# Pairs of feature tiles of the up projection by seven half-width block products, and sums of weights by adding DMAs

## The chip, the cores and the metric

The kernel runs on one core of one Trainium2 chip. The metric is the device time of one execution in microseconds (us). Five engines take part: TensorE (PE) multiplies matrices and loads its weights, VectorE (DVE) and ScalarE (ACT) work on elements, GpSimd (POOL) works on elements and can issue DMAs, SyncE (SP) issues most DMAs. Data lies in DRAM, in the on-chip memory SBUF, and in PSUM, to whose eight banks matmuls write.

## The reference

One post-norm layer of an encoder over 512 tokens of width 1024, in fp32. A combined projection of x feeds a bidirectional state-space branch and a dilated attention branch; both are projected back, gated and mixed, and the sum goes through a layer norm. The result, h1 here, enters the channel sublayer, which alone the change touches:

```python
h = layer_norm(alpha * h + mix, ln1_g, ln1_b)
f = jnp.square(jax.nn.relu(h @ w_up)) @ w_down
h = layer_norm(alpha * h + f, ln2_g, ln2_b)
```

w_up is 1024 × 4096, w_down is 4096 × 1024.

## The kernel before

fp32 products are made from three matmuls on split operands: each operand is a high part (a cast to the type fp32r, done by ACT) and a low part (the difference, done by DVE), and high × high, high × low and low × high are summed in PSUM.

**Up projection.** h1 is transposed (`h1_transpose`, L941 on) into `hth` and `htl`, high and low part, as eight K tiles of 128 features by 512 tokens. The 4096 features of the layer are 32 tiles of 128, in four chunks `ch` of eight tiles `b`. `up_block(ch, b)` makes one tile: `up_mm` issues 24 matmuls (eight K tiles, three products each) of 512 columns into one bank, through `quarters` (L141), with the weights stationary; then ACT takes relu (L993) and the square (L994) into r. The first half of tiles 0 to 3 of chunk 0 is made earlier, between the transposes, with 256 columns. The weights come from `Stream`: SP loads 512 KB per tile (`wraw`, three buffers, L89), ACT casts `wh` (L110), DVE subtracts `wl` (L111); wh and wl have two buffers each.

**Down projection.** For chunks 0 to 2 each chunk's part is a product of 2 × 2 blocks made by the seven products of Winograd's form of Strassen's method. `SEQ` gives their order, 1, 5, 6, 7, 3, 2, 4; `product` (L151 to L153) issues 24 matmuls of 512 columns for each. Some operands are sums of blocks: `sums` makes those of the activations (L1027) and those of the weights (L1030), both on DVE and in place in a block whose own use is over; `split` then makes high and low parts of activations (`ah`, `al`, L1036, L1037) and of weights (`ch`, `cl`, L1042, L1043), two buffers each. The weight blocks are four quarters of 1 MB (`wq`), loaded by `load_quarters` on SP. Chunk 3 is multiplied plainly at the end.

**Order.** In the loop one tile of chunk ch + 1 alternates with one product of chunk ch. All engines run their own queue in order; the program's text and a scheduler with priorities set those orders, and semaphores tie the queues together. A `tile_pool` with n buffers under one tag makes the writer of buffer n + 1 wait for the readers of the first.

The loop of before, in which the change lies:

```python
    for ch in range(3):
        for n, p in enumerate(SEQ):
            up_block(ch + 1, UP_ORDER[1][n])
            product(ch, p, ops)
            if n < 6:
                ops = prepare(ch, n + 1)
```

Of the kernel before, what the change touches and what calls it, by code (L numbers as in the profile page):

```python
# [45 lines left out]
def hybrid_layer_kernel(ctx: ExitStack, tc: tile.TileContext, t: dict, out: bass.AP):  # L46
# [29 lines left out]

    class Stream:
        def __init__(self):
            self.srcs, self.raw, self.hl, self.n = [], {}, {}, 0

        def add(self, ap, width=1024, hold=None):
            self.srcs.append((ap, width, hold))

        def load(self, i):
            if i < len(self.srcs) and i not in self.raw:
                ap, width, hold = self.srcs[i]
                r = wp.tile([P, 1024], F32, name=f"wraw{i}", tag="wraw", bufs=3)
                if i:
                    dma.dma_start(r[:, :width], ap)  # L89
                else:  # L90
                    act.dma_start(r[:, :512], ap[:, :512])
                    dma.dma_start(r[:, 512:width], ap[:, 512:])
                self.raw[i] = r

        def prep(self, i):
            if i < len(self.srcs) and i not in self.hl:
                self.load(i)
                ap, width, hold = self.srcs[i]
                if hold and hold[0] not in held:
                    return  # L100
                r = self.raw[i]
                if hold:
                    h = held[hold[0]].tile([P, 1024], F32R, name=f"wh{i}", tag=f"h{hold[1]}", bufs=1)
                    l = held[hold[0]].tile([P, 1024], F32R, name=f"wl{i}", tag=f"l{hold[1]}", bufs=1)
                else:
                    h = wp.tile([P, 1024], F32R, name=f"wh{i}", tag="wh", bufs=2)
                    l = wp.tile([P, 1024], F32R, name=f"wl{i}", tag="wl", bufs=2)
                with tc.high_priority(PRIO):
                    if i:
                        act.copy(h[:, :width], r[:, :width])  # L110
                        dve.tensor_sub(l[:, :width], r[:, :width], f32(h[:, :width]))  # L111
# [787 lines left out]
    for ch in range(4):  # L899
        for b in UP_ORDER[ch > 0]:  # L900
            if ch or b >= NU:
                ws.add(t["w_up"][ch * 8 + b])
# [52 lines left out]
    pre = []
# [44 lines left out]
    qp = wq_ctx.enter_context(tc.tile_pool(name="qp", bufs=1, side="right", reuse_waits="tile"))  # L1000
    quarter = {}

    def load_quarters(ch):
        for half, c in ((0, 0), (0, 1), (1, 1), (1, 0)):
            q = qp.tile([P, 2, 1024], F32, name=f"wq{ch}_{half}{c}", tag="wq", bufs=4)
            for j in range(2):
                dma.dma_start(q[:, j, :], t["w_dn"][ch // 2, c, (ch % 2) * 4 + half * 2 + j])
            quarter[ch, half, c] = q

    SEQ = [1, 5, 6, 7, 3, 2, 4]  # L1010

    def operands(ch, p):

        b11, b12, b22, b21 = [quarter[ch, *x] for x in ((0, 0), (0, 1), (1, 1), (1, 0))]
        lo, hi = slice(0, 256), slice(256, 512)
# [4 lines left out]
        w = {1: (b11, None), 5: (b11, (b12, b11)), 6: (b11, (b22, b11)), 7: (b12, (b22, b12)),  # L1020
             3: (b22, None), 2: (b21, None), 4: (b11, (b21, b11))}[p]
        return a, w

    def sums(ch, p):
        (a, asum), (w, wsum) = operands(ch, p)
        if asum:
            dve.tensor_tensor(a, asum[0], asum[1], op=asum[2])  # L1027
        if wsum:
            for j in range(2):
                dve.tensor_sub(w[:, j, :], wsum[0][:, j, :], wsum[1][:, j, :])  # L1030
# [206 lines left out]
```

## Time and profile before

| | |
|---|---|
| median of three runs | 1001.0 us (1000.8 to 1001.79) |
| profiled execution, span from first to last instruction | 999.2 us |
| the median lies above that span by | 1.8 us |
| PE busy | 988.5 us, 99 % |
| DVE busy | 742.2 us, 74 % |
| ACT busy | 553.6 us, 55 % |
| POOL busy | 51.3 us, 5 % |
| moved by DMA | 140.43 MB |
| granted TensorE clock | 0.998 |

The profile is one execution. The page gives busy times of the engines, the chain of waits that ended last, and groups of instructions by line; windows give the same for a stretch of time, and the timeline single instructions. A group's row reads: line, engine, operation, output <- inputs, shapes, count | busy us, mean ns of one | idle time of the engine just before them, and what ended it. A row of waits reads: who waited <- for whom: us in total, times, the longest. A row of the chain reads: start in us, length in us, engine, tile, line, count. A row of DMAs reads: destination <- source, the queue, count, size, median us from issue to landing.

The stage that the change touches lies, in that execution, between about 650 us (transposes of h1) and 948 us. The loop's three chunks begin at 708.8, 790.6 and 872.2.

### The profile page before, as it was taken

To read this page: it belongs to the slowest core of one execution; us is meant where nothing else is said; L and a number is where in the kernel's file an instruction comes from. 1 tells how busy PE (TensorE), PEld (TensorE's weight loads), DVE (VectorE), ACT (ScalarE), POOL (GpSimd) and SP (SyncE) were. 2 spreads that over 40 slices of the span, in tenths; PEclk is the share of its full clock that TensorE was granted. 3 is DMA by queue.
4 is the path that set the end of the run, shared out by engine and by line. 5 is a ranking of instruction groups with operands and counts; after the bars stand their busy time and mean duration, and the time that the engine had idled before them with its cause. 6 is when DMAs were issued, how large, how long until landed. Compare 5 with 4: busy or idle time off the path is not lost.

```text
span 999.2 us, 13445 instructions
## 1 busy us (share of the span) xinstructions
PE 988.5 (99%) x4967; PEld 820.6 (82%) x4967; DVE 742.2 (74%) x1120; ACT 553.6 (55%) x1031; POOL 51.3 (5%) x50
## 2 busy tenths in 40 slices
PE   9999999999999999999999999999999999999997
PEld 7888888888887888788778888898888888888886
DVE  4296997789998998895787267564775876787457
ACT  4454796469766984884774343134543545455330
POOL 0000100120012002102000000000000000000000
PEclk9999999999999999999999999999999999999999
DMA  7445376335653574484764258234224224321222
GB/s 243 153 134 167 105 216 196 96 118 153 204 148 113 165 221 123 119 256 142 250 204 117 75 189 312 68 101 153 73 96 153 80 72 145 100 61 45 85 85 85
DMA packets 53202, 140.43 MB, mean 141 GB/s; under 512 B 7056, under 2 KB 8208, under 8 KB 52880
## 3 DMA queue, kind: packets, MB, share of 16 engines
q1 hardware_dynamic: 52992, 139.30, 44.6%
q8 instruction: 39, 0.64, 0.3%
q10 hardware_dynamic: 144, 0.26, 0.1%
q14 instruction: 27, 0.22, 0.1%
HBM read 128.25 MB, written 11.30 MB: 140 GB/s over the span
## 4 chain that ended last, share of the span: by engine, by line
PE 96%; DVE 3%; ACT 0%; issue 0%; DVEq 0%; ACTq 0%
PE ps_u L141 18%; PE ps_pa L141 9%; PE ps_z L141 9%; PE ps_x L141 9%; PE ps_g L141 7%; PE ps_p L153 4%; PE ps_p L152 4%; PE ps_p L151 4%; PE ps_q L141 3%; PE ps_k L141 3%; PE ps_B L141 2%; PE ps_yo L526 2%; PE ps_C L141 2%; PE ps_d L152 1%; PE ps_d L151 1%; PE ps_d L153 1%
## 5 line engine op out<-in xcount | busy, mean ns | idle before, releaser
L111 DVE TENSOR_TENSOR wl<-wraw,wh 128x1024 fp32r<-128x1024 f32 (+1 forms) x141 | 173.6, 1235 | 140.7 <-ACT wh L110 114.8
L110 ACT CAST wh<-wraw 128x1024 fp32r<-128x1024 f32 (+1 forms) x141 | 146.1, 1040 | 195.1 <-PE ps_u L141 100.6
L141 PE MATMUL ps_u<-hth,wh 128*128 128x512 f32 (+1 forms) x272 | 101.4, 377 | 0.2 <-ACT hth L951 0.2
L141 PE MATMUL ps_u<-hth,wl 128*128 128x512 f32 (+1 forms) x272 | 101.2, 377 | 0.0
L1043 DVE TENSOR_TENSOR cl<-wq,ch 128x1024 fp32r<-128x1024 f32 x42 | 51.2, 1222 | 33.0 <-ACT ch L1042 33.0
L151 PE MATMUL ps_p<-ch,ah 128*128 128x512 f32 x168 | 65.4, 389 | 0.0
L152 PE MATMUL ps_p<-cl,ah 128*128 128x512 f32 x168 | 65.4, 389 | 0.0
L153 PE MATMUL ps_p<-ch,al 128*128 128x512 f32 x168 | 65.4, 389 | 0.0
L141 PE MATMUL ps_u<-htl,wh 128*128 128x512 f32 (+1 forms) x272 | 63.8, 377 | 0.0
L141 PEld LDWEIGHTS ps_u<-hth,wh 128*128 128x128 f32 x272 | 51.2, 188 | 9.8 <-ACT hth L951 0.5
L141 PEld LDWEIGHTS ps_u<-hth,wl 128*128 128x128 f32 x272 | 51.2, 188 | 9.4
L141 PEld LDWEIGHTS ps_u<-htl,wh 128*128 128x128 f32 x272 | 49.2, 188 | 9.4
L1042 ACT CAST ch<-wq 128x1024 fp32r<-128x1024 f32 x42 | 44.1, 1051 | 16.9 <-PE ps_p L153 16.9
L141 PE MATMUL ps_pa<-yh,wh 128*128 128x512 f32 x128 | 51.7, 404 | 0.0
L141 PE MATMUL ps_g<-xh,wh 128*128 128x512 f32 x128 | 51.5, 402 | 0.0
L141 PE MATMUL ps_z<-xh,wh 128*128 128x512 f32 x128 | 50.7, 396 | 0.0
L141 PE MATMUL ps_x<-xh,wh 128*128 128x512 f32 x128 | 50.4, 394 | 0.0
L141 PE MATMUL ps_z<-xl,wh 128*128 128x512 f32 x128 | 49.9, 390 | 0.0
L141 PE MATMUL ps_g<-xl,wh 128*128 128x512 f32 x128 | 49.9, 390 | 0.0
L141 PE MATMUL ps_x<-xl,wh 128*128 128x512 f32 x128 | 49.8, 389 | 0.0
L141 PE MATMUL ps_pa<-yl,wh 128*128 128x512 f32 x128 | 48.4, 393 | 0.0
L314 DVE SCALAR_TENSOR_TENSOR acc<-ps_x,vec,acc 128x510 f32<-128x510 f32 (+1 forms) x64 | 47.6, 744 | 0.8 <-ACT acc L312 0.3
(298 smaller groups left out, 2331.8 us busy)
## 6 DMA issues: line engine op xcount, KB each, us to landing
wraw<-in_w_in_dram SPq DMA_DIRECT2D x68, 512.0 KB, 3.7
bc<-dr_acr SPq DMA_DIRECT2D x64, 256.0 KB, 4.4
wraw<-in_w_up_dram SPq DMA_DIRECT2D x32, 512.0 KB, 3.6
wq<-in_w_dn_dram SPq DMA_DIRECT2D x24, 512.0 KB, 4.4
be<-dr_ear SPq DMA_DIRECT2D x32, 256.0 KB, 5.4
wraw<-in_w_ps_dram SPq DMA_DIRECT2D x16, 512.0 KB, 3.8
dr_gate<-g SPq DMA_DIRECT2D x16, 256.0 KB, 2.1
wraw<-in_w_out_dram SPq DMA_DIRECT2D x8, 512.0 KB, 4.6
```

The costliest lines, as they stand in the source:

```text
L110: act.copy(h[:, :width], r[:, :width])
L111: dve.tensor_sub(l[:, :width], r[:, :width], f32(h[:, :width]))
L141: ins = pe.matmul(ps, l, r, start=(first and n == 0), stop=(last and n == len(seq) - 1))
L151: pe.matmul(ps, lh, rh, start=(first and i == 0), stop=False)
L152: pe.matmul(ps, lh, rl, start=False, stop=False)
L153: ins = pe.matmul(ps, ll, rh, start=False, stop=(last and i == n - 1))
L314: dve.scalar_tensor_tensor(acc[:, o0:o1], ps[:, i0:i1], w(k), acc[:, o0:o1], op0=ALU.mult, op1=ALU.add)
L526: pe.matmul(po[d][:, ch(c)], prev[d, c][:, pr * P:(pr + 1) * P], C[:, ch(c)], start=True, stop=True)
L1042: act.copy(h, w[:, j, :])
L1043: dve.tensor_sub(l, w[:, j, :], f32(h))
```

## The change

**Up projection.** Tiles 0 to 7 (chunk 0) stay. Tiles 8 to 31 become twelve pairs (`PAIRS`: chunks 1 to 3, tiles 4 and 5, 6 and 7, 0 and 1, 2 and 3). A pair's product (512 tokens × 1024 by 1024 × 256 features) is seen as 2 × 2 blocks: A11 and A12 are K tiles 0 to 3 and 4 to 7 of the first 256 tokens, A21 and A22 the same of the last 256; B11 and B21 are the K halves of the pair's first tile, B12 and B22 of its second. It is made by seven products `qmul` of 12 matmuls of 256 columns, in four segments (`up_seg`):

- seg 0: x = A11·B11, y = A12·B21; C11 = x + y
- seg 1: z = S1·T1, x += S2·T2
- seg 2: x += S3·T3, z += S4·B22; C22 and C12 come from z, x and copies taken in between
- seg 3: x += A22·T4; C21 = x

with S1 = A21 − A22, S2 = S1 − A11, S4 = A12 + S2, S3 = A11 − A21, and T1 = B11 + B12, T3 = B12 + B22, T2 = T1 + B22, T4 = B21 + T2. The S are made once, in `act_sums` on DVE and ACT during chunk 0, from `hf`, an unsplit copy of h1 transposed (eight more copies on ACT, L957); S3 overwrites A21.

**Sums by DMA.** T1, T3, T2 and T4 are made in the raw weight buffers of a pair by four adding DMAs of 256 KB on POOL's queue (L1063, L1067, L1068, L1070; called adds A, B, C, D in this order), then split by `wsplit` (L1049 casts on ACT, subtractions on DVE) into three operand buffers. The third add may only start when T1 has been read, since it overwrites it. The weight sums of the down projection's products 5, 6, 7 and 4 become adding DMAs of 1 MB on POOL's queue (L1171); the signs of the activation sums and of some additions change with it.

**Order.** The order of PE in the loop is written out by hand: for the first pair of a chunk (q = 0) seg 0, seg 1, a product, seg 2, a product; for the next two seg 3 of the pair before, seg 0, half a product, seg 1, the other half, seg 2, a product; for the last seg 3, seg 0, half a product, seg 1, the other half, seg 2, seg 3. Products use two pairs of banks instead of three. The weight quarters' pool opens later, when `hf` is closed.

```diff
+    def act_sums():
+        a11, a12, a21, a22 = hf[:, 0:4, LO], hf[:, 4:8, LO], hf[:, 0:4, HI], hf[:, 4:8, HI]
+        s3 = fp.tile([P, 4, S], F32, name="s3", tag="r1", bufs=2)[:, :, LO]
+        dve.tensor_sub(s3, a11, a21)
+        dve.tensor_sub(a22, a21, a22)
+        act_split("S1", a22)
...
+    def pair_prep(n, e):
+
+        if n >= len(PAIRS):
+            return
+        r0, r1 = raw_w[n, 0], raw_w.get((n, 1))
+        if e == 0:
+            h, l = slot(f"pa{n}")
+            wsplit(h, l, r0)
+            op_w[n, "B11"], op_w[n, "B21"] = (h, l, K0), (h, l, K1)
+            pool.dma_start(r0[:, K0], r1[:, K0], accum_op=ALU.add)
+        elif e == 1:
+            h, l = slot(f"pb{n}")
+            wsplit(h[:, K0], l[:, K0], r0[:, K0])
+            pool.dma_start(r1[:, K0], r1[:, K1], accum_op=ALU.add)
+            pool.dma_start(r0[:, K0], r1[:, K1], accum_op=ALU.add)
+            wsplit(h[:, K1], l[:, K1], r0[:, K0])
+            pool.dma_start(r0[:, K1], r0[:, K0], accum_op=ALU.add)
+            op_w[n, "T1"], op_w[n, "T2"] = (h, l, K0), (h, l, K1)
...
+    def qmul(ps, a, n, w, first):
+        src, k0, cs = mov[a]
+        h, l, ws_ = op_w.pop((n, w))
+        seq = [(h, x, k) for k in range(4) for x in range(2)] + [(l, 0, k) for k in range(4)]
+        for i, (w_, x, k) in enumerate(seq):
+            wk = slice(ws_.start + k * P, ws_.start + (k + 1) * P)
+            pe.matmul(ps[:, LO], w_[:, wk], src[:, x, k0 + k, cs], start=(first and i == 0), stop=(i == 11), skip_group_check=not first)
...
     def sums(ch, p):
-        (a, asum), (w, wsum) = operands(ch, p)
+        (a, asum), (w, wadd) = operands(ch, p)
         if asum:
             dve.tensor_tensor(a, asum[0], asum[1], op=asum[2])
-        if wsum:
-            for j in range(2):
-                dve.tensor_sub(w[:, j, :], wsum[0][:, j, :], wsum[1][:, j, :])
+        if wadd is not None:
+            pool.dma_start(w, wadd, accum_op=ALU.add)
...
-    BANKS = [(0, 1), (3, 4), (5, 2)]
+    BANKS = [(0, 1), (3, 4)]
...
+    with tc.manual_schedule(engines={mybir.EngineType.PE}):
+        for c in range(3):
+            for q in range(4):
+                n = c * 4 + q
+                if q:
+                    up_seg(n - 1, 3)
+                up_seg(n, 0)
+                pair_prep(n, 2)
+                if q == 0:
+                    up_seg(n, 1)
+                    pair_prep(n, 3)
+                pr = product(c, SEQ[2 * q], ops)
+                next(pr)
+                if q:
+                    up_seg(n, 1)
+                    pair_prep(n, 3)
+                for _ in pr:
+                    pass
+                if q < 3:
+                    ops = prepare(c, 2 * q + 1)
+                pair_prep(n + 1, 0)
+                up_seg(n, 2)
```

On PE, at the boundary from chunk 0 to chunk 1 of the loop, the order of before has whole tiles (the end of tile 3 of chunk 1 and the beginning of tile 4 of chunk 2, whose weights are wh118 and wl118; rows that only repeat are left out):

```order
L141 MATMUL ps_u1_3_7266<-htl_6044,wh117_7196 128x512 x8
L141 MATMUL ps_u2_4_7315<-hth_6043,wh118_7269 128x512 [waits Activation_49]
L141 MATMUL ps_u2_4_7315<-hth_6043,wl118_7270 128x512 [waits DVE_49]
L141 MATMUL ps_u2_4_7315<-hth_6043,wh118_7269 128x512
L141 MATMUL ps_u2_4_7315<-hth_6043,wl118_7270 128x512
```

and the order of the change, at the same place, has seg 3 of pair 3 (pd3), seg 0 of pair 4 (pa4), seg 1 of pair 4 (pb4 holds T1 and T2) and product 1 of chunk 1 (here too without the rows that repeat):

```order
L1089 MATMUL ps_x3_7418<-ht_6049,pd3h_7497 128x256 [waits DVE_49]
L1089 MATMUL ps_x3_7418<-ht_6049,pd3l_7498 128x256 x4
L1089 MATMUL ps_x4_7600<-ht_6049,pa4h_7517 128x256 x8
L1089 MATMUL ps_y4_7613<-ht_6049,pa4h_7517 128x256 x8
L1089 MATMUL ps_z4_7636<-S1_6556,pb4h_7590 128x256 [waits DVE_49,Activation_49]
L1089 MATMUL ps_z4_7636<-S1_6556,pb4l_7591 128x256 [waits DVE_49]
L1089 MATMUL ps_x4_7600<-S2_6560,pb4h_7590 128x256 [waits Activation_49]
L1089 MATMUL ps_x4_7600<-S2_6560,pb4l_7591 128x256 [waits DVE_49]
L148 MATMUL ps_p11_3_7671<-ch110_7580,ah11_7576 128x512
```

The wait of a tile for its weights became two waits a product apart, and the product of T2 follows that of T1 with nothing between.

On ACT, at the same boundary, before (ch and ah are weights and activations of products 1 and 5 of chunk 1; wh119 and wh120 are weights of later tiles):

```order
L1042 CAST ch110_7303<-wq1_00_7254 128x1024 [waits DMAHW0_49,DVE_49,PE_49]
L1042 CAST ch111_7307<-wq1_00_7254 128x1024 [waits DMAHW1_49,DVE_49,PE_49]
L110 CAST wh119_7318<-wraw119_7194 128x1024 [waits DMAHW5_49,PE_49]
L993 ACTIVATE r1_0_7044<-ps_u1_3_7266 128x512
L994 ACTIVATE r1_0_7044<-r1_0_7044 128x512 [waits Activation_49]
L1036 CAST ah11_7299<-r1_0_7044 128x1024 [waits Activation_49]
L1036 CAST ah15_7380<-r1_0_7044 128x1024 [waits DVE_49]
L110 CAST wh120_7398<-wraw120_7267 128x1024 [waits DMAHW0_49,PE_49]
```

and with the change (pb4h is cast twice: first its half T1, in the first row, and last its half T2; pc4h is T3|B22; DMASW are semaphores of POOL's DMAs):

```order
L1049 CAST pb4h_7590<-pr4_0_7293 128x512 [waits DMASW4_49,PE_49]
L1102 ACTIVATE r1_0_7209<-r1_0_7209 128x512 [waits DVE_49]
L1103 ACTIVATE r1_0_7209<-r1_0_7209 128x512 [waits Activation_49]
L1141 ACTIVATE r1_0_7209<-ps_x3_7418 128x256 [waits PE_49]
L1049 CAST pc4h_7630<-pr4_1_7452 128x1024 [waits DMAHW1_49,DMASW5_49]
L1142 ACTIVATE r1_0_7209<-r1_0_7209 128x512 [waits Activation_49]
L1119 COPY v1_4_7626<-ps_x4_7600 128x256 [waits PE_49]
L1177 CAST ah11_7576<-r1_0_7209 128x1024 [waits Activation_49]
L1177 CAST ah15_7703<-r1_0_7209 128x1024 [waits DVE_49]
L1049 CAST pb4h_7590<-pr4_0_7293 128x512 [waits DMASW7_49]
```

The cast of T2 stands behind eight instructions that follow the cast of T1.

On POOL, where before issues no DMA, the adds of pair 4 (pr4_0 and pr4_1 are its raw weights) and the 1 MB sums of chunk 1's products 5 and 7 (wq1) stand in one row:

```order
L1063 DMA pr4_0_7293<-pr4_1_7452 128x512 [waits DMAHW1_49,DMAHW5_49,DMASW7_49,DVE_49]
L1067 DMA pr4_1_7452<-pr4_1_7452 128x512 [waits DMASW4_49,DMASW1_49]
L1171 DMA wq1_00_7550<-wq1_01_7553 128x2048 [waits DMAHW2_49,DMAHW3_49,DMAHW0_49,DVE_49]
L1068 DMA pr4_0_7293<-pr4_1_7452 128x512 [waits DVE_49]
L1171 DMA wq1_01_7553<-wq1_11_7556 128x2048 [waits DMAHW7_49,DMAHW6_49,DMASW6_49]
L1070 DMA pr4_0_7293<-pr4_0_7293 128x512 [waits DMASW7_49]
```

The add for T2 (L1068) stands behind a 1 MB add, and that for T4 (L1070) behind two.

More of the change, by code (lines that the diff above doesn't have):

```diff
@@ L84, in load @@
         def load(self, i):
-            if i < len(self.srcs) and i not in self.raw:
+            if i < len(self.srcs) and i not in self.raw and (self.end is None or i < self.end):
                 ap, width, hold = self.srcs[i]
@@ L95, in prep @@
         def prep(self, i):
-            if i < len(self.srcs) and i not in self.hl:
+            if i < len(self.srcs) and i not in self.hl and (self.end is None or i < self.end):
                 self.load(i)
@@ L897, in layer_norm @@
         dve.scalar_tensor_tensor(r, r, mv[:, 1:2], g[:, 1, :], op0=ALU.mult, op1=ALU.add)
[L899 to L902, printed above, removed]
+    for b in range(NU, 8):
+        ws.add(t["w_up"][b])
+    ws.end = len(ws.srcs)
     for c in range(2):
@@ L998, in hybrid_layer_kernel, with act_split @@
     wu_ctx.close()
+    LO, HI = slice(0, 256), slice(256, 512)
+    mov = {"A11": (ht, 0, LO), "A12": (ht, 4, LO), "A22": (ht, 4, HI), "S3": (ht, 0, HI)}
+    def act_split(name, src):
+        if name == "S3":
+            d = ht[:, :, 0:4, HI]
+        else:
+            d = fp.tile([P, 2, 4, 256], F32R, name=name)
+            mov[name] = (d, 0, slice(0, 256))
+        act.copy(d[:, 0], src)
+        dve.tensor_sub(d[:, 1], src, f32(d[:, 0]))
+    def act_sums():
[4 more added lines that the diff above has]
+        act_split("S1", a22)
+        dve.tensor_sub(a11, a22, a11)
+        act_split("S2", a11)
+        dve.tensor_add(a12, a12, a11)
+        act_split("S4", a12)
+        return s3
@@ new lines, in temp, with relu2, up_seg @@
+    def temp(name):
+        return fp.tile([P, 256], F32, name=name, tag=name[:2], bufs=1)
+    def relu2(r):
+        act.activation(r, r, AF.Relu)
+        act.activation(r, r, AF.Square)
+    def up_seg(n, seg):
+        if not 0 <= n < len(PAIRS):
+            return
+        ch, b = PAIRS[n]
+        if seg == 0:
+            if b % 4 == 0:
+                r2[ch, b // 4] = fp.tile([P, 4, S], F32, name=f"r{ch}_{b // 4}", tag=f"r{b // 4}", bufs=1 + b // 4)
+            px[n] = [bank((6, 7)[n % 2], f"ps_x{n}"), None, None]
+            x = px[n][0]
+            qmul(x, "A11", n, "B11", True)
+            px[n][1] = y = bank(5, f"ps_y{n}")
+            qmul(y, "A12", n, "B21", True)
+            v1 = temp(f"v1_{n}")
+            act.copy(v1, x[:, LO])
+            dve.tensor_add(half(n, 0, LO), y[:, LO], v1)
+            act.activation(half(n, 0, LO), half(n, 0, LO), AF.Relu)
+        elif seg == 1:
+            px[n][2] = z = bank(2, f"ps_z{n}")
+            x = px[n][0]
+            qmul(z, "S1", n, "T1", True)
+            qmul(x, "S2", n, "T2", False)
+            v5, v2 = temp(f"v5_{n}"), temp(f"v2_{n}")
+            act.copy(v5, z[:, LO])
+            act.activation(v2, x[:, LO], AF.Copy, scale=-1.0)
+            px[n] += [v5, v2]
+        elif seg == 2:
+            x, _, z, v5, v2 = px[n]
+            qmul(x, "S3", n, "T3", False)
+            qmul(z, "S4", n, "B22", False)
+            dve.scalar_tensor_tensor(half(n, 1, HI), x[:, LO], -1.0, v5, op0=ALU.mult, op1=ALU.add)
+            dve.tensor_add(half(n, 1, LO), z[:, LO], v2)
+            relu2(half(n, 1, slice(0, S)))
+        else:
+            x = px.pop(n)[0]
+            qmul(x, "A22", n, "T4", False)
+            act.activation(half(n, 0, HI), x[:, LO], AF.Relu)
+            act.activation(half(n, 0, slice(0, S)), half(n, 0, slice(0, S)), AF.Square)
@@ L1063, in product @@
         ah, al, wc = ops
-        pss = [bank(n, f"ps_p{ch}{p}_{n}") for n in BANKS[npr[0] % 3]]
+        pss = [bank(n, f"ps_p{ch}{p}_{n}") for n in BANKS[npr[0] % 2]]
         npr[0] += 1
```

138 lines of the change are left out of this document (98 added, 40 removed).

## The prediction

> **What bounds the kernel now.** I read the page's head, the clock, the chain of waits and then the windows of the stage that changes.
>
> ```profile
> span 999.2 us, 13445 instructions
> PE 988.5 (99%) x4967; PEld 820.6 (82%) x4967; DVE 742.2 (74%) x1120; ACT 553.6 (55%) x1031; POOL 51.3 (5%) x50
> ...
> PE 96%; DVE 3%; ACT 0%; issue 0%; DVEq 0%; ACTq 0%
> ```
> ```profile
> core 0: 999.2 us, clock 0.998
> ```
> ```profile
> core 0: us, PE busy (x) PEld busy (x) DVE busy (x) ACT busy (x) POOL busy (x), PEclk, DMA share, GB/s
> 650.00:668.00 18.00, 17.76 (x130) 16.51 (x129) 14.54 (x23) 4.89 (x10) 0.00 (x0) 1.00 0.18 58
> 668.00:708.80 40.80, 40.80 (x193) 34.27 (x192) 17.17 (x15) 19.52 (x26) 0.00 (x0) 1.00 0.49 155
> 708.80:790.60 81.80, 81.80 (x362) 67.73 (x361) 61.50 (x64) 40.13 (x47) 0.00 (x0) 1.00 0.31 103
> 790.60:872.20 81.60, 81.60 (x361) 67.57 (x361) 61.30 (x64) 40.13 (x47) 0.00 (x0) 1.00 0.33 104
> 872.20:948.40 76.20, 76.20 (x337) 63.09 (x337) 53.79 (x57) 36.80 (x44) 0.00 (x0) 1.00 0.20 62
> ```
> TensorE (PE) sets the end: 96 % of the chain, at a granted clock of 0.998, and in the three windows of one chunk each that begin at 708.8 it never pauses. Any matmul time removed there is gained, any wait put there is paid in full. The waits of that stage say who follows whom:
>
> ```profile
> ACT wh L110 <- PE ps_u L141: 74.5, 23, 4.4
> ...
> ACT ah L1036 <- PE ps_p L152: 18.9, 15, 1.4
> ACT ch L1042 <- PE ps_p L153: 16.9, 24, 1.7
> ```
> ScalarE (ACT) waits for PE, never the other way round: weights are split long before they are used. The profiled execution spans 999.2 us; the median 1001.0 lies 1.8 above it. I sum against 999.2 and add 1.8.
>
> **The change part by part.**
>
> *Matmuls.* Twelve pairs of feature tiles fall from 48 matmuls of 512 columns to 84 of 256.
>
> ```profile
> 657.14 2.87 PE ps_u L141 x24
> ...
> 714.44 5.44 PE ps_u L141 x24
> ```
> The chain shows both widths: 24 matmuls of 512 columns take 5.44 us (226.7 ns each); the first halves of tiles 0 to 3, 24 matmuls of 256 columns, take 2.87 us (119.6 ns, above half of 226.7). A pair was 48 × 0.2267 = 10.88 us and is 84 × 0.1196 = 10.05; 12 × 0.83 = **10.0 us removed**. At exactly half it would be 12 × (10.88 − 9.52) = 16.3, which the 2.87 row excludes. One product of a pair (12 matmuls) is 1.435 us.
>
> *ACT and DVE on average.* Prices:
>
> ```profile
> L111 DVE TENSOR_TENSOR wl<-wraw,wh 128x1024 fp32r<-128x1024 f32 x22 | 26.9, 1225 | 29.3 <-ACT wh L110 29.2
> L1030 DVE TENSOR_TENSOR wq<-wq,wq 128x1024 f32<-128x1024 f32 x20 | 24.0, 1220 | 0.1
> L110 ACT CAST wh<-wraw 128x1024 fp32r<-128x1024 f32 x22 | 23.2, 1055 | 73.7 <-PE ps_u L141 73.7
> ...
> L994 ACT ACTIVATE r<-r 128x512 f32<-128x512 f32 x22 | 14.0, 634 | 0.7
> ...
> L993 ACT ACTIVATE r<-ps_u 128x512 f32<-128x512 f32 x22 | 12.9, 588 | 0.0
> ```
> ```profile
> L609 DVE TENSOR_TENSOR yl<-y,yh 128x512 fp32r<-128x512 f32 x16 | 11.0, 688 | 1.2 <-ACT yh L608 0.5
> L608 ACT CAST yh<-y 128x512 fp32r<-128x512 f32 x16 | 8.7, 619 | 0.0
> L529 DVE TENSOR_TENSOR be<-be,ps_yo 128x256 f32<-128x256 f32 x16 | 6.6, 414 | 0.0
> ```
> ```profile
> L780 ACT COPY tn<-ps_pn 128x256 f32<-128x256 f32 x4 | 1.5, 370 | 2.4 <-PE ps_pn L775 2.4
> ```
> VectorE (DVE) loses, per chunk, eight low-part subtractions and eight weight sums (16 × 1.22 = 19.5); a pair adds subtractions of 1.22 twice and 0.69 three times and three of 0.41 on half a tile: 5.74, or 23.0 per chunk. 61.3 − 19.5 + 23.0 = 64.8 of the new 81.6 − 3.3 = 78.3 us: 83 %. ACT loses 8 × (1.06 + 0.59 + 0.63) = 18.2 and gains per pair casts (2 × 1.06, 3 × 0.62), three copies of 0.37 and 2.6 of relu and square, 7.7: 40.1 − 18.2 + 30.8 = 52.7, 67 %. Both have room; waits can only come from the order.
>
> *Adding DMAs.* The trace has no DMA from GpSimd's queue (POOL), none inside SBUF and none that adds. Nearest rows:
>
> ```profile
> wraw<-in_w_up_dram SPq DMA_DIRECT2D x32, 512.0 KB, 3.6
> wq<-in_w_dn_dram SPq DMA_DIRECT2D x24, 512.0 KB, 4.4
> be<-dr_ear SPq DMA_DIRECT2D x32, 256.0 KB, 5.4
> ...
> dr_gate<-g SPq DMA_DIRECT2D x16, 256.0 KB, 2.1
> ...
> ga<-dr_gate SPq DMA_DIRECT2D x8, 256.0 KB, 3.9
> ...
> out_dram<-h SPq DMA_DIRECT2D x8, 256.0 KB, 2.0
> ```
> ```profile
> q1 hardware_dynamic: 52992, 139.30, 44.6%
> ```
> The queue moved 139.30 MB in 44.6 % of 999.2 us, 312 GB/s while busy: 0.84 us for 256 KB, 3.36 for 1 MB. Call L the time from issue to landing of a 256 KB add: from 2.0 (plain store) to 5.4 (the slowest 256 KB row). An add reads two operands; I take a store plus a second pass, 2.1 + 0.84 = **L 2.9**. For 1 MB, L2: the fixed part 2.1 − 0.84 = 1.26 plus one pass (4.6) or two (8.0); I take the middle, **L2 6.3**, also near what two wq loads in a row would suggest (4.4 + 1.9).
>
> [...]
>
> *Pair 0.* Let T be the end of the last block of chunk 0 on PE (703.6). PE then runs A11·B11 and A12·B21 (to 2.87), S1·T1 (to 4.30), S2·T2 (to 5.74). The buffer for B11|B21 comes free at T − 5.4; cast, subtraction, and the first add issues at T − 2.5, landing T + 0.4. T1 is cast by 2.1 and its low part done at 2.9, which releases the third add (it overwrites what T1 was read from): it lands at 2.95 + 2.9 = 5.9. T2's cast ends at 6.5, its subtraction, behind others of DVE, at 7.55; the last four matmuls then end at 8.06 instead of 5.74: **2.3 us of stall**, growing one for one with L.
>
> *Chunk boundaries (pairs 4 and 8).* Here S1·T1 comes before any product, not behind half of one as in the other pairs. Count from the end of S2·T2 of pair 3. PE: half a product to 2.72, S3·T3 and S4·B22 to 5.59, A22·T4 to 7.03, the next pair's seg 0 to 9.90, S1·T1 to 11.33, S2·T2 to 12.77. ACT casts B11|B21 by 1.1, DVE finishes at 2.3, add A lands 2.4 + 2.9 = 5.3. T1 must wait for an operand buffer that seg 2 still reads: cast 5.62 to 6.2, low part 6.85. Add C then goes 6.9 to 9.8, or, if the 1 MB add for the next chunk's product 5 that was queued before it (5.4) is served first, 5.4 + 6.3 + 0.84 = 12.5. T2's cast is last in ACT's row: relu and squares, T3|B22 (waits for the second add, 8.3; done 9.35), square 9.9, copy 10.15, ah of product 1 to 11.15, ah of product 5 after DVE's sum at 11.75, so to 12.83; T2 13.3. DVE: al of product 1 to 12.9, the y add 13.2, al of product 5 14.4, T2's low part 14.95. PE needed T2 at 11.33; the low matmuls start at 14.98 and S2·T2 ends at 15.46 rather than 12.77: **2.7 us, twice**. At L = 2.1 it stays 2.0 or more, since ACT and DVE are what is late; above 2.9 each boundary grows by two for each us of L, since adds A and B stand in series ahead of the cast of T3|B22. These row times of ACT rest on how soon it follows PE:
>
> ```profile
> 785.19 1.06 ACT L110 CAST wh<-wraw 128x1024 fp32r<-128x1024 f32 x1 [4.38 <-PE ps_u L141]
> 786.15 0.59 ACT L993 ACTIVATE r<-ps_u 128x512 f32<-128x512 f32 x1
> ...
> 793.35 1.06 ACT L1042 CAST ch<-wq 128x1024 fp32r<-128x1024 f32 x1 [0.51 <-PE ps_p L153]
> ```
> (next instruction 0.1 before the printed end of the last.)
>
> *Product 6.* Its weights b11 + b22 are added into the buffer that product 5 was split from. From the start of product 1: DVE is done with product 5's weights at 9.5, the add is issued at 9.55; cast and subtraction need 2.3 more and PE is there at 18.3. It stalls only if L2 is over 6.4; at 6.3 **nothing**. The sums of products 5, 7 and 4 have more time.
>
> *Hidden parts.* Pairs 1 to 3, 5 to 7 and 9 to 11 have half a product (2.72 us) between seg 0 and S1·T1 and came out 0.7 to 7 us early by the same count: 0. Eight copies of 0.59 into hf stand on ACT, where 4.9 of the 18 us of 650 to 668 are used; the operand sums of S1 to S4 (about 8 × 1.22 on DVE, 4 × 1.05 on ACT) go into 668 to 708.8, where DVE is busy 17.2 of 40.8 and ACT 19.5: 0. If that cover were gone they would cost up to 9.8.
>
> *Sum:* −10.0 + 2.3 + 2 × 2.7 = −2.3; 999.2 − 2.3 + 1.8 = **998.7 us**.
>
> **The rivals.**
> - **B, the 1 MB adds read twice.** With L2 = 8.0, product 6 is late by 1.6 in each of three chunks (4.8), and at the two boundaries the third add, served behind a 1 MB one, lands at 14.24, which ends S2·T2 0.8 later (1.6): 998.7 + 6.4 = 1005.1, slower. It decides from L2 6.4, has eaten the gain at 7.2 and is over 0.2 % slower at 7.6. For: two operands must be read, and the rows' own 1 MB pass is already 3.36. Against: stores of 256 KB land in 2.0, and SP's queue is only a third busy here.
> - **C, T2 is not late.** The scheduler's row for ACT is fixed but my instants may be too late, above all at the boundaries where one early sum moves three casts. Without the waits 999.2 − 10.0 + 1.8 = 991.0; with half of them about 995. For: PE never waited for ACT in the old loop. Against: T2 needs three splits and two adds in series, and PE has 1.4 us between T1 and T2.
> - **D, adds begin late.** If a POOL issue waits out a DVE instruction of 1.22 (83 % busy), L is 4.1 and L2 7.5: pair 0 3.5, boundaries 5.1 each, product 6 3 × 1.1: 17.0 of stall, 999.2 − 10.0 + 17.0 + 1.8 = 1008.0. No row tells: POOL is idle in all three windows.
>
> [...]
>
> **How the numbers follow.** A difference under 0.2 % (2 us) can't be told from none here. The forecast A has 0.50, with a range of its own of 996 to 1002.5 (L 2.1: stalls of 1.5 + 2 × 2.0; L 3.6: 3.0 + 2 × 4.1): faster 0.28, same 0.20, slower 0.02. B has 0.24 (same 0.04, slower 0.20), C 0.14 (faster), D 0.12 (slower). Faster 0.42, same 0.24, slower 0.34. The range 993 to 1007 holds A and B, half of C and the nearer edge of D.
>
> **What would show it.** Right: matmuls of 256 columns at 119 to 120 ns; PE idle only before S2·T2 of pairs 0, 4 and 8, released by ACT or DVE at the T2 split, 2 to 3 us each; adds of 256 KB landing in about 2.9 us. Wrong: PE waiting before product 6 (B), waits in the pairs inside a chunk, or adds of more than 4 us (D); PE as closed as before (C). A matmul of 256 columns at over 10.88 / 84 = 129.5 ns would take away the gain whole.

## The result, and the profile after

The changed kernel takes 1027.2 us (median; 1025.9 to 1030.8), the kernel before 1001.4 in the same runs: a ratio of 1.026, 95 % interval 1.025 to 1.028. It is slower by 26 us, where 998.7 was forecast and 1007 was the top of the range. The page's head, the chain and the clock of the changed kernel:

```profile
span 1025.4 us, 14690 instructions
PE 991.2 (97%) x5399; PEld 841.0 (82%) x5399; DVE 758.8 (74%) x1176; ACT 589.8 (58%) x1127; POOL 103.0 (10%) x110
...
PE 75%; DMA 12%; DVE 6%; issue 4%; ACT 2%; POOL 1%; SPq 0%; DVEq 0%; POOLq 0%; ACTq 0%
```
```profile
core 0: 1025.4 us, clock 0.985
```

TensorE (PE) had 96 % of the chain and a clock of 0.998; it has 75 % now, adding DMAs have come into the chain, and the mean clock is lower. PE's waits from 640 us on, where before had one of 0.2 us:

```profile
PE ps_x L1089 <- ACT pb4h L1049: 7.0, 1, 7.0
PE ps_x L1089 <- ACT pb8h L1049: 6.8, 1, 6.8
PE ps_p L148 <- ACT ch L1183: 3.0, 3, 1.8
PE ps_x L1089 <- ACT pb0h L1049: 3.0, 1, 3.0
PE ps_p L149 <- DVE cl L1184: 2.6, 4, 0.8
```

pb0h, pb4h and pb8h are T2 of pairs 0, 4 and 8: the places are those of the forecast. ch and cl are product 6's weights (and once product 5's).

**A ledger of the loop.** From the first matmul behind chunk 0 (before: of the loop's first tile, which ends where the first product begins, at 708.8; after: of pair 0) to the first of the plain chunk at the end, the timeline has 244.8 us before (703.39 to 948.19) and 269.8 after (704.30 to 974.11). Without any wait it would be 235.2: 84 segments of 1.435 us, which is what a segment takes wherever nothing is waited for, and 21 products of 5.46. So the removal of matmuls is real (9.6 us), and 34.6 us have come in, called the excess. By the times between the starts of segments they lie so:

| place | forecast | measured |
|---|---|---|
| pair 0, S2·T2 | 2.3 | 4.5 |
| pair 4 | 2.7 | 9.9 |
| pair 8 | 2.7 | 8.8 |
| product 6, in the three chunks | 0 | 1.7, 2.3, 5.8 |
| elsewhere | 0 | 1.6 |

By kind they are 22.3 us of idle PE, 9.2 us lost by work at a lower clock (the sum over windows of 2 us of busy time × (1 − clock)), and 3.1 that neither shows. The windows around pair 4 show the second kind:

```profile
792.00:794.00 2.00, 1.94 (x17) 1.74 (x15) 0.00 (x0) 0.39 (x2) 1.25 (x2) 1.00 1.07 197
794.00:796.00 2.00, 0.00 (x0) 0.00 (x0) 1.07 (x1) 2.00 (x4) 0.00 (x0) 1.00 1.10 225
796.00:798.00 2.00, 0.00 (x0) 0.00 (x0) 2.00 (x3) 1.31 (x2) 0.00 (x0) 0.63 1.10 229
...
802.00:804.00 2.00, 2.00 (x10) 1.98 (x10) 0.73 (x1) 0.96 (x2) 0.00 (x0) 0.50 1.09 205
804.00:806.00 2.00, 2.00 (x6) 1.53 (x5) 1.89 (x2) 0.36 (x2) 0.00 (x0) 0.50 1.08 174
806.00:808.00 2.00, 2.00 (x8) 1.58 (x8) 0.47 (x1) 0.00 (x0) 0.00 (x0) 0.81 0.78 223
```

(The columns are those of the windows in the prediction.) PE stands from 793.9 to 800.9. The mean clock of 0.63 in the window from 796 puts the fall to 0.50 at 796.5, 2.6 us into the wait; that of 0.81 in the window from 806 puts the return to 1.00 at 806.8, 5.8 us after PE works again.

**Why T2 of pair 4 is late.** POOL's row at that place, and of ACT's row the two casts that wait for it (pc4h for add B, pb4h for add C) and the instruction just ahead of the second:

```profile
785.79 0.86 POOL L1063 DMA_DIRECT2D pr<-pr  x1 [7.69 <-DVE h L1223]
790.61 0.86 POOL L1067 DMA_DIRECT2D pr<-pr  x1 [3.96 <-DMA pr<-pr]
791.20 1.16 POOL L1171 DMA_DIRECT2D wq<-wq  x1
791.80 1.45 POOL L1068 DMA_DIRECT2D pr<-pr  x1
799.24 0.86 POOL L1171 DMA_DIRECT2D wq<-wq  x1 [5.99 <-DMA wq<-wq]
```
```profile
793.85 1.04 ACT L1049 CAST pc4h<-pr 128x1024 fp32r<-128x1024 f32 x1 [1.61 <-DMA pr<-pr]
...
797.32 1.05 ACT L1177 CAST ah<-r 128x1024 fp32r<-128x1024 f32 x1 [0.69 <-DVE r L1169]
800.25 0.62 ACT L1049 CAST pb4h<-pr 128x512 fp32r<-128x512 f32 x1 [1.88 <-DMA pr<-pr]
```

Add A (L1063) is issued at 785.8, add B (L1067) waits for it to 790.6, and behind B the 1 MB add of product 5 leaves at 791.2, 0.6 us ahead of add C (L1068), which makes T2. C lands only at 800.2, 8.4 us after its issue and 1.3 after the 1 MB add (791.20 + 7.75). But C is only the last part of the wait: ACT's own row, which add B had held up to 793.85, is done with what stands ahead of T2's cast at 798.4, and stands idle for C for the last 1.9 us (1.88 here, 1.87 at pair 8). The medians from issue to landing:

```profile
wq<-wq POOLq DMA_DIRECT2D x12, 1024.0 KB, 7.9
pr<-pr POOLq DMA_DIRECT2D x48, 256.0 KB, 3.5
```

### The profile page after: what moved, and what is told of

It reads as the page before. It is cut to its first block, busy times and chain, and to the rows that moved or that the text cites. A ratio compares the mean times of both kernels' runs of the same rounds, so it can differ in the third digit from the quotient of the medians.

```text
span 1025.4 us, 14690 instructions
## 1 busy us (share of the span) xinstructions
PE 991.2 (97%) x5399; PEld 841.0 (82%) x5399; DVE 758.8 (74%) x1176; ACT 589.8 (58%) x1127; POOL 103.0 (10%) x110
## 4 chain that ended last, share of the span: by engine, by line
PE 75%; DMA 12%; DVE 6%; issue 4%; ACT 2%; POOL 1%; SPq 0%; DVEq 0%; POOLq 0%; ACTq 0%
PE ps_pa L138 9%; PE ps_z L138 9%; PE ps_x L138 9%; PE ps_g L138 7%; DMA pr<-pr 6%; DMA wq<-wq 4%; PE ps_q L138 3%; PE ps_k L138 3%; PE ps_x L1089 2%; PE ps_u L138 2%; PE ps_B L138 2%; PE ps_yo L529 2%; PE ps_C L138 2%; DMA pr<-in_w_up_dram 2%; PE ps_p L149 1%
## 5 line engine op out<-in xcount | busy, mean ns | idle before, releaser
L108 DVE TENSOR_TENSOR wl<-wraw,wh 128x1024 fp32r<-128x1024 f32 (+1 forms) x117 | 144.1, 1236 | 104.8 <-ACT wh L107 79.5
L107 ACT CAST wh<-wraw 128x1024 fp32r<-128x1024 f32 (+1 forms) x117 | 120.9, 1037 | 105.7 <-PE ps_vb L150 16.5
L148 PE MATMUL ps_p<-ch,ah 128*128 128x512 f32 x168 | 67.8, 404 | 3.0 <-ACT ch L1183 3.0
L149 PE MATMUL ps_p<-cl,ah 128*128 128x512 f32 x168 | 68.0, 405 | 2.6 <-DVE cl L1184 2.6
L498 ACT ACTIVATE U<-bc,acr 128x128 f32<-128x128 f32 x128 | 42.4, 391 | 11.1 <-DMA bc<-dr_acr 7.5
L500 DVE SCALAR_TENSOR_TENSOR U<-bc,acr,U 128x128 f32<-128x128 f32 x128 | 42.0, 364 | 0.6 <-ACT U L498 0.6
L138 PE MATMUL ps_u<-ht,wh 128*128 128x512 f32 (+1 forms) x160 | 41.7, 348 | 0.2 <-ACT ht L955 0.2
L504 ACT ACTIVATE G<-cb,tok 128x128 f32<-128x128 f32 x128 | 41.8, 391 | 0.0
L148 PEld LDWEIGHTS ps_p<-ch,ah 128*128 128x128 f32 x168 | 32.9, 196 | 9.8 <-ACT ch L1183 3.7
L149 PEld LDWEIGHTS ps_p<-cl,ah 128*128 128x128 f32 x168 | 32.8, 195 | 9.7 <-DVE cl L1184 3.9
```

The source lines that it names most:

```text
L138: ins = pe.matmul(ps, l, r, start=(first and n == 0), stop=(last and n == len(seq) - 1))
L148: pe.matmul(ps, lh, rh, start=(first and i == 0), stop=False)
L149: pe.matmul(ps, lh, rl, start=False, stop=False)
L498: act.activation(U[:, ch(c)], bb[:, ch(c)], AF.Identity, bias=acr[:, c, 32 + h:33 + h])
L500: dve.scalar_tensor_tensor(U[:, ch(c)], bf[:, ch(c)], acr[:, c, h:h + 1], U[:, ch(c)], op0=ALU.subtract, op1=ALU.min)
L504: act.activation(G1[:, ch(c)], cb[0][:, c, :], AF.Copy, scale=tok[:, c, h:h + 1])
```

## The experiments

Times are medians; "before" is the kernel before in the same runs (1001.4 to 1001.7). "Loop" and "excess" are those of the ledger; in 3 and 9 they hold 67 and 30 filling matmuls of 0.227 us (15.2 and 6.8 us). The rows of the single kernels come from one execution each.

| kernel | us | ratio to before, interval | loop | excess over 235.2 |
|---|---|---|---|---|
| changed | 1027.2 | 1.026, 1.025 to 1.028 | 269.8 | 34.6 |
| 1, third add ahead of the 1 MB add | 1020.2 | 1.019, 1.017 to 1.020 | 261.8 | 26.6 |
| 2, weight sums on DVE | 1012.6 | 1.010, 1.008 to 1.013 | 257.2 | 22.0 |
| 3, waits filled with matmuls | 1034.4 | 1.033, 1.031 to 1.034 | 277.5 | 42.3 |
| 4, the pairs' sums on DVE | 999.2 | 0.9975, 0.9964 to 0.9986 | 242.1 | 6.9 |
| 5, all sums on DVE | 1001.6 | 1.000, 0.999 to 1.001 | 244.6 | 9.4 |
| 6, DVE only where the add was late | 1008.1 | 1.006, 1.005 to 1.008 | 250.8 | 15.6 |
| 7, the pairs' and product 6's sums on DVE | 994.5 | 0.993, 0.992 to 0.994 | 237.4 | 2.2 |
| 8, kernel before with 1 MB adds | 1001.7 | 1.000, 0.999 to 1.001 | | |
| 9, as 2, with filled waits | 1004.9 | 1.004, 1.002 to 1.005 | 247.7 | 12.5 |
| 10, as 7, T1 of pair 0 in a free buffer | 992.4 | 0.991, 0.990 to 0.993 | 235.8 | 0.6 |

### 1: the third add ahead of the 1 MB add

```diff
-                    ops = prepare(c, 7)
+                    ops = split(c + 1, SEQ[0]) if c < 2 else None
                 pair_prep(n + 1, 1)
+                if q == 3 and c < 2:
+                    _, l, ws_ = op_w[n + 1, "T1"]
+                    w = quarter[c + 1, 0, 0][:, 0, 0:1]
+                    dve.scalar_tensor_tensor(w, f32(l[:, 0:1]), 0.0, w, op0=ALU.mult, op1=ALU.add)
+                    sums(c + 1, SEQ[1])
```

The small operation adds nothing to one column of the weights that product 5's 1 MB add writes, but reads T1's low part; so that add has to wait for T1's low part, as add C does, and it now leaves behind C.

> At the two chunk boundaries the third adding DMA of pairs 4 and 8 is issued ahead of the 1 MB add of the next chunk's product 5 (which is made to wait for T1's low part by one small operation of DVE); nothing else is changed by intent. Theory Q (the 1 MB add ahead in the queue delays T2): the third add lands 3.5 us after its issue at about 791.8 instead of 8.4, T2 is cast at about 797, PE's wait there falls from 7.0 to about 3.3 us, twice, and with it some of the time at the halved clock: 1027.2 becomes 1015 to 1020. Rival A (ACT's and DVE's rows are what is late, as in the prediction): the wait stays at 6 us or more, 1025 or more.

```profile
PE ps_p L148 <- ACT ch L1183: 3.9, 2, 2.1
PE ps_x L1089 <- ACT pb4h L1049: 3.2, 1, 3.2
PE ps_x L1089 <- ACT pb8h L1049: 3.1, 1, 3.1
```

These are PE's waits in the loop. Those of pairs 4 and 8 fall from 7.0 and 6.8 to 3.2 and 3.1, the size that theory Q gives. But two things have changed, as the rows of pair 4 show:

```profile
791.60 0.86 POOL L1068 DMA_DIRECT2D pr<-pr  x1 [0.32 <-DVE wq L1304]
```
```profile
795.33 1.05 ACT L1177 CAST ah<-r 128x1024 fp32r<-128x1024 f32 x1
796.27 0.62 ACT L1049 CAST pb4h<-pr 128x512 fp32r<-128x512 f32 x1
797.07 1.05 ACT L1177 CAST ah<-r 128x1024 fp32r<-128x1024 f32 x1 [0.17 <-DVE r L1169]
```

Add C lands 3.4 us after its issue, at 795.0. T2's cast no longer waits for it: it starts at 796.3, behind ACT's own row, and one place further forward, ahead of ah of product 5. In the old place it could not have begun before that cast of ah ends, at about 798.0. So of the 3.7 us some 1.9 are the idle time for C that the changed kernel shows, hence the 1 MB add ahead of it, and some 1.8 the new place in ACT's row. The 3.2 that are left are ACT's row behind add B. The time, 1020.2, is at the edge of what was expected: PE reaches product 6 earlier and waits longer there (1.9 and 2.1 us against 0.9 and 1.8).

### 2: weight sums on DVE

```diff
-        if wadd is not None:
+        if wadd is not None and p in (5, 6, 7, 4):
+            for j in range(2):
+                dve.tensor_add(w[:, j, :], w[:, j, :], wadd[:, j, :])
+        elif wadd is not None:
             pool.dma_start(w, wadd, accum_op=ALU.add)
```

> The down projection's weight sums go back to DVE (two additions of 128x1024 a product, 8 a chunk); the pairs keep their adding DMAs. Theory Q with B (1 MB adds are the trouble, in the queue and before product 6): waits at pairs 4 and 8 fall to about 3.5 us each, those before product 6 (5.6 us in all, with the first product 6 at 1.1) go, and most of the halved clock: 1008 to 1013. Rival (DVE has no room for 9.8 us more in a chunk of 78, it would be 95 % busy): new waits of PE for DVE, 1020 or more.

```profile
PE ps_x L1089 <- ACT v L1129: 4.2, 2, 2.2
PE ps_x L1089 <- ACT pb0h L1049: 3.2, 1, 3.2
PE ps_x L1089 <- ACT pb4h L1049: 2.6, 1, 2.6
PE ps_x L1089 <- ACT pb8h L1049: 1.5, 1, 1.5
```

No 1 MB add is left, and no wait before product 6. T2 of pairs 0, 4 and 8 is still late by 1.5 to 3.2 us, with only 256 KB adds (3.3 us in the median) in the queue: this is the size that was forecast for pairs 4 and 8 (2.7). T2's cast has the forward place of experiment 1 here too. New are two waits, of 2.0 and 2.2 us, for the copy that frees x before S3·T3 of pairs 5 and 9. Together with 1, the boundary's 7 us come apart into about 3 for the chain of adds and splits, 1.8 for the place of T2's cast in ACT's row, and 1.9 for the 1 MB add.

### 3 and 9: waits filled with matmuls

```diff
...
             qmul(z, "S1", n, "T1", True)
+            if n % 4 == 0:
+                pad = bank(BANKS[npr[0] % 2][0], f"ps_pad{n}")
+                for i in range(11 if n == 0 else 28):
+                    pe.matmul(pad, ht[:, 0, i % 8, 0:P], ht[:, 0, 4 + i % 4, :], start=True, stop=True)
```

> As the changed kernel, with matmuls of 512 columns that nothing reads put between S1*T1 and S2*T2 of pairs 0, 4 and 8: 11, 28 and 28 of them (2.5, 6.3 and 6.3 us at full clock), so PE works through most of its wait. Theory H (the clock is halved because PE stood idle): the granted clock stays 1.00 at these three places, and 1.3 + 2.9 + 1.9 = 6.1 us are gained though more is computed: about 1021. Rival N (the clock falls for another reason, the short matmuls or the load as a whole): the clock falls as before and the time is 1027 or more.

The clock did what theory H said: it stayed at 1.00 through the three places, and S2·T2 took 1.54 us at pair 4 instead of 2.73. The time did not: 1034.4. The order of ACT had changed with the longer row of PE: T4's cast now stood ahead of the copy that frees x for S3·T3, and T4's add stands, as in the changed kernel, behind a second 1 MB add. ACT's row and PE's wait there:

```profile
812.21 0.62 ACT L1049 CAST pd4h<-pr 128x512 fp32r<-128x512 f32 x1 [9.54 <-DMA pr<-pr]
812.73 1.04 ACT L1049 CAST pa5h<-pr 128x1024 fp32r<-128x1024 f32 x1
813.68 0.38 ACT L1135 ACTIVATE v<-ps_x 128x256 f32<-128x256 f32 x1
```
```profile
PE ps_x L1089 <- ACT v L1135: 9.5, 2, 4.8
```

So its time tells nothing of H, though the clock does: it fell at these new waits of 4.8 and 4.7 us instead, and at two of product 6. Experiment 9 fills the waits of kernel 2, where no 1 MB add can make T4 late (12, 10 and 8 matmuls for pairs 0, 4 and 8).

> The kernel with the weight sums on DVE (no 1 MB adds, the pairs' adds by DMA), and in it 12, 10 and 8 matmuls of 512 columns that nothing reads between S1*T1 and S2*T2 of pairs 0, 4 and 8 (2.7, 2.3 and 1.8 us), where PE had waited 3.2, 2.6 and 1.5 us. Theory H (the clock is halved after PE stood idle): the clock is 1.00 through the whole loop and the 6.2 us of work at a lower clock come back: 1012.6 becomes 1005.5 to 1008. Rival N (not idleness): the clock falls as before and the time is 1012 or more.

1004.9 against 1012.6: more is computed and 7.7 us are gained. The windows of 9 around pair 4's S2·T2, where kernel 2 worked at a clock of 0.50 for 6 us:

```profile
790.00:792.00 2.00, 2.00 (x15) 1.83 (x14) 1.59 (x2) 2.00 (x4) 0.59 (x1) 1.00 0.36 65
792.00:794.00 2.00, 2.00 (x13) 1.76 (x12) 2.00 (x3) 1.83 (x4) 0.27 (x1) 1.00 0.56 84
794.00:796.00 2.00, 1.85 (x12) 1.52 (x11) 1.97 (x3) 0.12 (x1) 0.00 (x0) 1.00 0.91 258
```

In the whole loop of 9 no work is done at a lower clock (6.2 us were lost by it in kernel 2). H holds. The gain is not the clock alone: the filling takes 6.8 us where the three waits had taken 7.2, and the two waits for copies (4.2) are gone, while 2.9 us of idle PE are left.

### 4 and 5: the pairs' sums on DVE, and all sums on DVE

```diff
-            pool.dma_start(r0[:, K0], r1[:, K0], accum_op=ALU.add)
+            dve.tensor_add(r0[:, K0], r0[:, K0], r1[:, K0])
...
-            pool.dma_start(r0[:, K0], r1[:, K1], accum_op=ALU.add)
+            dve.tensor_add(r0[:, K0], r0[:, K0], r1[:, K1])
```

(the other two alike; 5 has the edit of 2 as well)

> The pairs' sums T1, T3, T2, T4 are made by DVE (four additions of 128x512 a pair, 0.69 us each, 11 us a chunk); the 1 MB adds stay. Theory: the chain of adding DMAs, each of 3.3 to 4.3 us from issue to landing and the third behind a 1 MB one, makes T2 late; without it the waits before S2*T2 of pairs 0, 4 and 8 (16.8 us) go with their share of the halved clock (6.1): about 1004 to 1008, with the waits before product 6 as they were. Rival (DVE, at 64.8 + 11 = 76 of 78 us a chunk, becomes the bound): waits move to DVE, 1015 or more.

```profile
PE ps_p L149 <- DVE cl L1184: 2.9, 6, 0.8
PE ps_x L1089 <- ACT pb0h L1049: 0.6, 1, 0.6
PE ps_x L1089 <- DVE pb0l L1050: 0.5, 1, 0.5
```

The waits of pairs 4 and 8 are gone, that of pair 0 is 1.1 us, the clock is 1.00 throughout. 999.2 us is below what was expected (1004 to 1008): product 6 also waits less, 1.5 us in all instead of 5.3, since in the last two chunks its add leaves 9.5 us after the start of product 1, as the forecast had it, and not 12.6 and 12.5. One edit turns a kernel slower than before into one that is 0.25 % faster.

> No adding DMA at all: the pairs' sums and the weight sums both on DVE (the products of pairs alone). Theory W (the adds' time to land is the trouble, not DVE's work): the excess over 235.2 us in the loop stays under that with the pairs' sums alone on DVE (6.9 us), so 994 to 1000. Rival L (DVE at 64.8 + 9.8 + 11 = 85.6 us a chunk is over the 78.3 that PE needs): about 7 us more per chunk, 1012 to 1022.

1001.6 lies between the two ranges. Its windows, of about a chunk each:

```profile
706.00:787.00 81.00, 79.90 (x513) 72.73 (x512) 79.35 (x103) 50.25 (x75) 0.00 (x0) 1.00 0.32 104
787.00:867.00 80.00, 77.55 (x488) 69.84 (x487) 79.12 (x101) 47.79 (x72) 0.00 (x0) 1.00 0.32 106
```

DVE is busy 79.1 of 80 us, 99 %, so it is the bound now, but a milder one than 7 us a chunk: 9.4 in all, for it has about 79 us of work in a chunk and not 85.6. The adding DMAs of 1 MB do earn something once DVE is full (7 below keeps three of four: 994.5); those of 256 KB did in none of these runs.

### 6: DVE only where the add had been late

```diff
+    def accum(n, d, a):
+        if n % 4:
+            pool.dma_start(d, a, accum_op=ALU.add)
+        else:
+            dve.tensor_add(d, d, a)
...
-        if wadd is not None:
+        if wadd is not None and p in (6,):
+            for j in range(2):
+                dve.tensor_add(w[:, j, :], w[:, j, :], wadd[:, j, :])
+        elif wadd is not None:
             pool.dma_start(w, wadd, accum_op=ALU.add)
```

> DVE adds only where the adding DMA was waited for: the sums of pairs 0, 4 and 8 and the weight sum of product 6 (12 x 0.69 us and 6 x 1.22 us in all); all other sums stay adding DMAs. Theory: pair 0 keeps 1.6 us as with all pairs' sums on DVE, pairs 4 and 8 and product 6 wait for nothing, the clock stays 1.00: 990.3 + 1.6 + about 1 in the span, 993 to 995 us. Rival (the moved work makes DVE's row late elsewhere, or 256 KB adds behind 1 MB ones become late in the other pairs): 997 or more.

A miss, and the rival held: 1008.1. PE now waits for T2 of the next pairs, 5 and 9:

```profile
PE ps_x L1095 <- ACT pb9h L1049: 5.0, 1, 5.0
PE ps_x L1095 <- ACT pb5h L1049: 4.6, 1, 4.6
```

and POOL's row tells why:

```profile
791.86 0.86 POOL L1180 DMA_DIRECT2D wq<-wq  x1 [7.20 <-DMA wq<-wq]
793.46 0.86 POOL L1056 DMA_DIRECT2D pr<-pr  x1 [0.74 <-DVE pa5l L1050]
802.45 0.86 POOL L1056 DMA_DIRECT2D pr<-pr  x1 [8.12 <-DMA pr<-pr]
808.45 0.86 POOL L1180 DMA_DIRECT2D wq<-wq  x1 [5.14 <-DVE cl L1193]
809.05 1.15 POOL L1056 DMA_DIRECT2D pr<-pr  x1
816.90 0.86 POOL L1056 DMA_DIRECT2D pr<-pr  x1 [6.69 <-DMA pr<-pr]
```

Pair 5's first add leaves 1.6 us after a 1 MB add and lands after 8.7 us (793.46 to about 802.2), its third leaves 0.6 after another and lands after 7.6. In the changed kernel the third was nearly as slow (6.9), the first was not (3.5: it left 10.6 us after the 1 MB add ahead of it). But PE had lost 12.2 us there, at pair 4 and before product 6, and began S2·T2 of pair 5 at 829.7, 5.2 us after the third add had landed. One wait had hidden the next.

### 7 and 10: a version that beats both

7 has the pairs' sums (4) and product 6's weight sum on DVE; the weight sums of products 5, 7 and 4 stay adding DMAs.

> All the pairs' sums and the weight sum of product 6 on DVE, the other 1 MB sums by DMA. Theory: the waits before product 6 (2.5 us in all in the run with the pairs' sums on DVE) go, those of product 7 for its low parts (2.3 us) stay or grow with DVE's load: 996 to 999. Rival: DVE at 78 of 78 us a chunk is late everywhere, 1003 or more.

994.5 us, below the 996 to 999 that were expected: PE's waits for low parts of product 7 are gone as well, though DVE is busy 76 of 80 us. The only waits left of PE in the loop are those of pair 0, the same 0.6 and 0.5 us as in 4.

10 deals out the operand buffers from the second one on:

```diff
-    slot_n = [0]
+    slot_n = [1]
```

> As the run with the pairs' sums and product 6's weight sum on DVE (994.5 us), and the three operand buffers are dealt out from the second one on, so that T1 of pair 0 goes to a buffer that is free from the start and not to one that the last tile of chunk 0 still reads. Theory: the last 1.6 us of wait, before S2*T2 of pair 0, came from that buffer; T2 is ready in time and 992.5 to 993.5 is left. Rival (DVE's and ACT's rows are what is late there): 994 to 995.

992.4 us, 0.9 % below before, and PE never waits in the loop, with DVE at 75 of 79 us:

```profile
703.00:782.00 79.00, 79.00 (x507) 72.12 (x506) 75.02 (x98) 49.00 (x74) 1.50 (x2) 1.00 0.38 120
782.00:861.00 79.00, 79.00 (x509) 72.24 (x509) 75.15 (x98) 50.25 (x77) 2.77 (x4) 1.00 0.51 147
```

The pairs of seven products are worth what they remove: the loop is 9.0 us shorter than before, and so is the time.

### 8: the kernel before with the 1 MB adds alone

The edit is that of `operands`, `sums` and the signs in `product`; the up projection stays as before.

> The kernel before with only the weight sums of the down projection changed to adding DMAs of 1 MB (with the signs of sums that go with it); the up projection is as before. Theory: product 6 alone is late, its weights being ready (8.0 + 0.3 + 3.3 us) after the low part of product 5's weights, where PE gives it 11.3 us: 0 to 1.5 us a chunk, 1001.6 to 1006. Rival (adding DMAs disturb more than that, or DVE's relief helps PE): outside of it.

1001.7, the same as before, and no wait of PE in the loop. An add takes as long as in the changed kernel:

```profile
wq<-wq POOLq DMA_DIRECT2D x12, 1024.0 KB, 7.8
```

By itself the change of the weight sums costs nothing and gives nothing: DVE's relief is not needed there, and no short chain of adds shares the queue.

## Why the prediction was wrong

**Right.** The matmuls: 1.435 us per segment, 9.6 us gained in the loop of 10.0 forecast (a product also grew from 5.44 to 5.46). Of the three places named for T2 every one waited. At pair 0, where no 1 MB add is near, add C landed 6.0 us after T (704.30 to 710.27), and 5.9 was counted; of the 4.5 us lost there PE waited 3.0, and the clock did the rest. The hidden parts (copies into hf, operand sums of S) cost nothing: from the first transpose of h1 to the end of chunk 0 PE takes 53.6 us in both kernels. The bound on product 6 was right for the first chunk: a stall if L2 is over 6.4, and at a landing of 7.7 us (724.36 to 732.1) product 6 lost 1.7. In the other two chunks the add was issued 3 us later than counted (12.6 and 12.5 us after the start of product 1, not 9.55), behind a product 1 that ran in part at half the clock, so that adds of 6.9 and 7.5 us were late as well.

**Wrong, the step on add C at the boundaries**, "or, if the 1 MB add ... is served first, 5.4 + 6.3 + 0.84 = 12.5", still ahead of ACT's own row at 12.83. C is served last, but it landed at 17.9 on that count (800.2 − 782.3): the 1 MB add could not leave at 5.4, since POOL's row is in order and add B, ahead of it, waited for A to land (8.9 instead); and it took 7.75, not 6.3. A itself was issued 1.1 us later than counted and took 4.3. That moved ACT's row too: T3|B22 waited for add B to 11.6, not 8.3, and the row was free for T2's cast at 16.1, not 12.83. The cast began at 18.0. Of the 5.1 us by which that is late, 3.26 came from A by way of B and ACT's row, and 1.88 from the 1 MB add ahead of C. So the wait was 7, not 2.7. Without the 1 MB add there, 3.2 and 2.6 are left (experiments 1 and 2, with the cast one place further forward); without the adds of 256 KB, nothing (4). In the terms of the sum: the boundaries came to 18.7 us instead of 5.4, pair 0 to 4.5 instead of 2.3, and product 6 to 9.8 instead of nothing.

**Wrong by size, L and L2.** 3.5 us where 2.9 was taken, 7.9 where 6.3 was. L2 lies at the two-pass end of the forecast's own bounds (8.0); whether an add makes two passes, no run shows. The fastest adds of 256 KB took 3.2.

**Wrong, a term that was missing**: the clock. 9.2 us of the excess are time lost by work at a lower clock behind waits, and the forecast priced a wait at its own length only. The third product 6 shows the worst of it: waits of 1.75 and 0.77 us, 5.8 us lost.

**The rivals.** B named both effects, a 1 MB add of 8.0 us that makes product 6 late and holds up the third add, and priced them at 1005 because it kept the early issue and the full clock. D's L2 (7.5) came near, its L (4.1) is as far from 3.5 as the forecast's 2.9, and its reason is not seen: an issue took 0.86 us, and up to 1.45 right behind another issue, with DVE busy 64 of 90 us a chunk (changed kernel), and 0.86 with 76 of 80 (experiment 7). C did not come true: T2 was late at all three places.

**What was right for the wrong reason.** That pairs inside a chunk would wait for nothing held in the changed kernel, but for pairs 5 and 9 by luck: PE came late from the boundary. With that wait gone they waited 4.6 and 5.0 us (experiment 6).

## What to carry to other kernels

Count a chain of DMAs by the queue that issues it: one that needs the result of another, or overwrites what it reads, waits for its landing and holds up all that stand behind it in the row (in the changed kernel POOL stood 3.96 us for that ahead of add B of pair 4, and 7.17 ahead of add D of pair 1), and one issued close behind a long transfer landed only after it here (8.4 us instead of 3.5). Then carry each late landing on into the rows of the other engines: ACT's row came late by 3.3 us in that way. An adding DMA is cheap where nothing waits for it soon (weights of a product far ahead) and dear on a chain of short sums, where an engine with a few free microseconds does the same in 0.7 us instead of 3.5. Price a wait of TensorE at its length plus the slow matmuls behind it (in the loops of the changed kernel and of experiments 2, 3 and 6 every wait of 2.5 us or more brought the clock down to 0.50, and so did some of 1.0 to 1.8 us with one of 0.7 or 0.8 close behind, while two of 2.0 and 2.2 did not), and take a removed wait as gained only after the next one in line has been looked at.

## What the runs showed of the hardware

- An adding DMA inside SBUF, issued by POOL, took 3.5 us from issue to landing for 256 KB (median of 48 in the changed kernel; 3.2 at best) and 7.9 for 1 MB (median of 12): 4.4 us more for 0.75 MB more, 5.9 us per MB. A plain pass of 1 MB would be 3.36 us, an estimate from the rate of SP's queue in the kernel before (312 GB/s while busy).
- A 256 KB add issued close behind a 1 MB add landed after it: seven times in the changed kernel, issued 0.6 to 1.3 us behind and landing 1.3 to 2.2 us after it (8.4 us from its issue at pair 4). Whether the order of the queue or the sharing of the DMA engines does it, no run separates.
- The granted clock fell to 0.50 in the three long waits of the changed kernel, 2.4, 2.6 and 3.9 us into waits of 3.0, 7.0 and 6.8, and the work behind them ran at it for 2.9, 5.8 and 3.9 us. With the one at the third product 6, the loop has four stretches at 0.50, of 3.4, 10.2, 6.8 and 6.8 us. Shorter waits ended differently: 1.75 + 0.77 us brought the clock down in the changed kernel and 1.50 + 0.66 in experiment 2, while single waits of 2.0 and 2.2 us in experiment 2 did not. What decides between them was not shown.
